# Gated scan heads: both directions as two planes of one tile per stream, queries read through a strided view

## The chip, the core and the metric

The kernel runs on one core of one Trainium2 chip. The metric is the device time of one execution in microseconds (us), the median of several runs; less is better. A profile of one execution gives the span of its instructions and what every engine did in it: PE is TensorE (matrix products), PEld its loading of weights, DVE is VectorE (elementwise work on tensors), ACT is ScalarE (activation functions, also copies), POOL is GpSimd and SP is SyncE, which here only issues DMAs.

## What is computed

Two layers of a backbone work on two streams of 256 tokens with 1024 features each: the context (its constant conditioning) and the latents. A layer is half an FFN step, a mixer with four groups of heads (differential attention, latent attention, a bidirectional gated scan, grouped attention with rotary positions) and another half FFN step. The last layer needs the context only as far as the latents read it. The change touches the scan alone. With q the queries, k the keys and logf the logarithms of the gates of one direction, a head of the scan is

```
def step(S, blk):
    qb, kb, vb, gb = blk
    G = jnp.cumsum(gb, axis=2)
    rel = jnp.where(tri, G[:, :, :, None, :] - G[:, :, None, :, :], -jnp.inf)
    att = jnp.einsum("bhtsk,bhsk->bhts", qb[:, :, :, None, :] * jnp.exp(rel), kb)
    o = jnp.einsum("bhts,bhsv->bhtv", att, vb) + jnp.einsum("bhtk,bhkv->bhtv", qb * jnp.exp(G), S)
    ...
o_f, st_f = _chunk_scan(q, fw[0], v, fw[1], s_f)
o_b, st_b = _chunk_scan(flip(q), flip(bw[0]), flip(v), flip(bw[1]), s_b)
return o_f + flip(o_b), st_f, st_b
```

that is, attention in which the product of query t and key s is weighted per feature by the product of all gates between them, once forward and once backward, and the latents go on from the state that the context left. There are four such heads per layer, with 128 features for queries and keys.

## The kernel before

Activations lie with features on the 128 partitions and the 512 tokens (context first, N = 512, S = 256) along the free axis. Dense weights are split into two parts of a shorter format, so a dense product takes three matmuls.

**The scan head** (`hgrn_head`, lines 769 to 891) computes the weighted attention as plain products. For levels b = 1, 2, 4, 8, 16, 32, 64 it takes pairs of neighbouring blocks of b tokens: queries of one block meet keys of the other, and both carry the product of the gates up to their common border. KF, KB, QF and QB are the keys and queries of the forward and of the backward direction, each a tile of 128 x 512. At a level below 32, ScalarE first copies the parts of them that meet into two tiles, MQ and MK: every second run of b elements comes from the backward tile, the others from the forward tile. TensorE multiplies MK and MQ in blocks of 32 x 32 (16 matmuls in layer 0, which the profile counts as 32), VectorE merges the blocks, which multiplies half of each of the four tiles by gate products T (`tensor_mul` in place), makes the next T for each direction, and a masked copy (`copy_predicated`) takes the level's part of the products into a tile attc. At levels 32 and 64 TensorE reads KF, KB, QF and QB themselves.

```
nc.scalar.activation(v(MQ, c0)[:, :, 0], v(QB, c0)[:, :, 0], AF.Copy)
nc.scalar.activation(v(MQ, c0)[:, :, 1], v(QF, c0)[:, :, 1], AF.Copy)
nc.scalar.activation(v(MK, c0)[:, :, 0], v(KF, c0)[:, :, 0], AF.Copy)
nc.scalar.activation(v(MK, c0)[:, :, 1], v(KB, c0)[:, :, 1], AF.Copy)
...
blocks(ps, MK, MQ)
...
nc.vector.tensor_mul(v(QF, c0)[:, :, 1], v(QF, c0)[:, :, 1], tv(TF, 0, c0))
```

Each of these instructions covers 256 elements per partition in layer 0. In layer 1 the queries of the context are not needed (c0 = 256), so copies and query merges cover 128, while the key merges still cover 256.

**The gates** (`hgrn_gate`, line 752, called from `hgrn` in `dense`, line 1227) come from the dense projections: Exp, a minimum, Ln and Exp give the sigmoid, layer 1 adds an affine step, and the keys are a product; each instruction covers 512 tokens.

**Order of the work.** `mixer` (line 1026) gives the dense products of a layer and all chains of dependent steps (head groups, attention units, scan heads) to a planner, `Weave` (line 101). It adds up a rough cost of what each engine got (`Engine.price`), runs a step of a chain when its inputs should be ready by a margin, up to four chains at a time in layer 0 and three in layer 1, and otherwise a piece of dense work. A scan head gives way at each level (the `yield` statements). `copy` (line 269) puts a copy from PSUM on ScalarE or on VectorE, whichever the planner's clocks say is behind. Then each engine works through its own queue in that order. A head's scan products use a pool of two PSUM banks, its tiles a pool of 36 slots. All instructions are issued by the helper `Engine`, so the profile puts every one of them on line 88, and the program's names tell them apart: hg0~g are tiles of a scan head of layer 0 (MQ, MK, QF, QB and others), hg0~ps its products in PSUM, hg0~T its gate products, mixin0~g the gates and keys; hg1 and mixin1 are those of layer 1.

## Time and profile before

| what | value |
|---|---|
| runs | 1996.98, 1991.06 and 1992.38 us; median 1992.38 |
| span of the profiled execution | 1989.2 us (its own time is not given apart from it) |
| busy in the span | TensorE 1943.7, VectorE 1332.2, ScalarE 908.3, GpSimd 0.2 us |
| first mixer, its scan and attention part | 410 to 775 us of the span |
| FFNs between the mixers | from 775 us on; the next stage after 1148 us |
| second mixer | 1519 to 1795 us |

A span is read from first to last instruction; the time of a run also holds what lies around it. Busy time counts an engine as busy while an instruction of it executes. [...] The releaser of a wait is the event that came last by the profile.

### The profile page before, as it was taken

The page shows a single profiled execution, that of the slowest core. Times are in us where ns is not written, and L with a number is a line of the kernel's source. Part 1 is how long each engine was busy: PE and PEld are TensorE (multiplying, and loading weights), DVE is VectorE, ACT ScalarE, POOL GpSimd, SP SyncE. Part 2 cuts the span into 40 slices and gives each one's busy share as a digit, 9 for nine tenths or more (in the row PEclk, how much of TensorE's full clock was granted, in tenths as well). Part 3 has the DMA queues.
Part 4 walks back from the last instruction along what each step waited for, and adds up shares of the span by engine and source line. Part 5 has one row for each costly group of instructions (what it writes and reads, how often), then busy time and mean ns, then how long its engine had stood idle before and what let it go on. Part 6 is the DMA issues. An engine that isn't in the chain of part 4 may idle for free.

```text
span 1989.2 us, 30652 instructions
## 1 busy us (share of the span) xinstructions
PE 1943.7 (98%) x11929; PEld 1612.7 (81%) x11929; DVE 1332.2 (67%) x2706; ACT 908.3 (46%) x1826; POOL 0.2 (0%) x4
## 2 busy tenths in 40 slices
PE   6999999999999799999999999999999999899999
PEld 5888888897777578888888898888889877689999
DVE  5688678465768957875477467676656577876554
ACT  4332223355778775322223343222235577875443
POOL 0000000000000000000000000000000000000000
PEclk9999999999999999999999999999999999999999
DMA  8565556423011102654554335465543312125564
GB/s 281 173 200 179 175 172 185 124 80 119 23 62 33 45 28 80 193 162 141 159 181 147 118 107 178 150 191 156 157 121 120 109 49 70 44 85 161 167 196 123
DMA packets 87600, 260.82 MB, mean 131 GB/s; under 512 B 9248, under 2 KB 21280, under 8 KB 87456
## 3 DMA queue, kind: packets, MB, share of 16 engines
q1 hardware_dynamic: 87456, 258.88, 41.6%
q8 instruction: 93, 1.52, 0.3%
q14 instruction: 51, 0.42, 0.1%
HBM read 257.79 MB, written 1.05 MB: 130 GB/s over the span
## 4 chain that ended last, share of the span: by engine, by line
PE 92%; ACT 3%; DVE 2%; DMA 1%; issue 0%; SPq 0%; DVEq 0%; ACTq 0%
PE ffn01~pa L88 12%; PE ffn10~pa L88 12%; PE ffn00~pa L88 10%; PE mixin0~pa L88 7%; PE ffn11~pa L88 6%; PE mixin1~pa L88 5%; PE ffn00~ps L88 3%; PE ffn10~ps L88 3%; PE ffn01~ps L88 3%; PE ffn00~pb L88 3%; PE ffn10~pb L88 3%; PE ffn01~pb L88 3%; PE mixo0~pa L88 2%; PE ffn11~pb L88 2%; PE ffn11~ps L88 2%; PE hg0~ps L88 1%
## 5 line engine op out<-in xcount | busy, mean ns | idle before, releaser
L88 ACT ACTIVATE ffn10~whi<-ffn10~raw 128x1024 fp32r<-128x1024 f32 (+1 forms) x76 | 72.0, 950 | 165.6 <-PE ffn10~pa L88 46.7
L88 ACT ACTIVATE ffn01~whi<-ffn01~raw 128x1024 fp32r<-128x1024 f32 (+1 forms) x76 | 72.0, 950 | 165.4 <-PE ffn01~pa L88 50.6
L88 ACT ACTIVATE ffn00~whi<-ffn00~raw 128x1024 fp32r<-128x1024 f32 (+1 forms) x73 | 68.7, 945 | 171.2 <-DMA ffn00~raw<-win 69.9
L88 PE MATMUL ffn01~pa<-mixo0~xh,ffn01~whi 128*128 128x512 f32 (+1 forms) x384 | 142.7, 373 | 1.2 <-ACT mixo0~xh L88 1.2
L88 PE MATMUL ffn01~pa<-mixo0~xl,ffn01~whi 128*128 128x512 f32 (+1 forms) x384 | 142.8, 372 | 0.0
L88 PE MATMUL ffn10~pa<-ffn01~xh,ffn10~whi 128*128 128x512 f32 (+1 forms) x384 | 142.6, 373 | 0.0
L88 PE MATMUL ffn10~pa<-ffn01~xl,ffn10~whi 128*128 128x512 f32 (+1 forms) x384 | 142.5, 372 | 0.0
L88 PE MATMUL ffn01~pa<-mixo0~xh,ffn01~wlo 128*128 128x512 f32 (+1 forms) x384 | 142.5, 372 | 0.0
L88 PE MATMUL ffn10~pa<-ffn01~xh,ffn10~wlo 128*128 128x512 f32 (+1 forms) x384 | 142.3, 372 | 0.0
L88 DVE TENSOR_TENSOR ffn10~wlo<-ffn10~raw,ffn10~whi 128x1024 fp32r<-128x1024 f32 (+1 forms) x76 | 82.1, 1083 | 69.5 <-ACT ffn10~whi L88 69.1
L88 DVE TENSOR_TENSOR ffn01~wlo<-ffn01~raw,ffn01~whi 128x1024 fp32r<-128x1024 f32 (+1 forms) x76 | 82.1, 1083 | 64.7 <-ACT ffn01~whi L88 64.2
L88 DVE TENSOR_TENSOR ffn11~wlo<-ffn11~raw,ffn11~whi 128x1024 fp32r<-128x1024 f32 (+2 forms) x80 | 82.5, 1038 | 58.4 <-ACT ffn11~whi L88 58.4
L88 DVE TENSOR_TENSOR ffn00~wlo<-ffn00~raw,ffn00~whi 128x1024 fp32r<-128x1024 f32 (+1 forms) x73 | 78.5, 1077 | 62.4 <-ACT ffn00~whi L88 62.3
L88 PE MATMUL ffn00~pa<-init~xh,ffn00~whi 128*128 128x512 f32 x304 | 118.8, 391 | 0.0
L88 PE MATMUL ffn00~pa<-init~xh,ffn00~wlo 128*128 128x512 f32 x304 | 118.4, 389 | 0.0
L88 PE MATMUL ffn00~pa<-init~xl,ffn00~whi 128*128 128x512 f32 x304 | 118.3, 389 | 0.0
L88 DVE SCALAR_TENSOR_TENSOR ada~g<-ffn00~adaw,cs,ada~g 128x512 f32<-128x512 f32 x168 | 115.0, 749 | 0.0
L88 ACT ACTIVATE ffn11~whi<-ffn11~raw 128x1024 fp32r<-128x1024 f32 (+2 forms) x80 | 72.4, 910 | 64.1 <-issue 29.9
L88 PE MATMUL ffn11~pa<-mixo1~xh,ffn11~whi 128*128 128x256 f32 x352 | 99.2, 283 | 2.1 <-ACT mixo1~xh L88 2.1
L88 PE MATMUL ffn11~pa<-mixo1~xl,ffn11~whi 128*128 128x256 f32 x352 | 99.5, 283 | 0.0
L88 PE MATMUL ffn11~pa<-mixo1~xh,ffn11~wlo 128*128 128x256 f32 x352 | 99.3, 283 | 0.0
L88 DVE SCALAR_TENSOR_TENSOR ada~g<-ffn01~adaw,cs,ada~g 128x512 f32<-128x512 f32 x140 | 95.8, 748 | 0.8 <-DMA ffn01~adaw<-ada_w 0.8
(567 smaller groups left out, 5190.9 us busy)
## 6 DMA issues: line engine op xcount, KB each, us to landing
ffn00~adaw<-ada_w SPq DMA_DIRECT2D x48, 512.0 KB, 3.7
ffn01~raw<-win SPq DMA_DIRECT2D x44, 512.0 KB, 4.0
ffn10~raw<-win SPq DMA_DIRECT2D x44, 512.0 KB, 3.8
ffn11~raw<-win SPq DMA_DIRECT2D x44, 512.0 KB, 4.2
ffn00~raw<-win SPq DMA_DIRECT2D x41, 512.0 KB, 4.3
ffn01~adaw<-ada_w SPq DMA_DIRECT2D x40, 512.0 KB, 3.8
ffn10~adaw<-ada_w SPq DMA_DIRECT2D x40, 512.0 KB, 3.7
norm00~adaw<-ada_w SPq DMA_DIRECT2D x16, 512.0 KB, 6.1
```

The lines of the kernel that those rows point to most:

```text
L88: return f(*a, **k)
```

## The change

It keeps gates, keys and queries of a head in tiles of two planes, one per direction, and one such tile per stream of 256 tokens: FF (gates), KK (keys) and QQ (queries; here the backward direction is the first plane). A view `skew(t, b)` takes every second run of b elements from the second plane and the others from the first, so what MQ and MK held is now one view of QQ or KK. The queries are read by TensorE through that view and are not copied any more. The keys are still copied, one copy per stream that is needed: two of 256 elements in layer 0 and one of 256 in layer 1. The merges, too, go through the view: one for the keys and one for the queries of each stream, 256 elements each. Both directions' T are one tile and one product. The gates' last step, the keys, the sum of the keys k0 and the first query products are made per stream, in halves. `view`, a new helper, builds an access pattern by hand. Comments and docstrings are removed; this is left out here.

```diff
+    def view(self, t, off, *dims):
+        return bass.AP(t.tensor, t.offset + off, [t.ap[0], *dims])
...
-        nc.scalar.activation(f, f, AF.Exp, scale=-1.0)
+        for o, cc in outs or [(f, slice(None))]:
+            nc.scalar.activation(o, f[:, cc], AF.Exp, scale=-1.0)
...
         if l:
-            nc.vector.scalar_tensor_tensor(k, k, a, f, ALU.mult, ALU.mult)
-            nc.scalar.activation(f, f, AF.Identity, bias=b, scale=a)
+            self.sigmoid(e, f, ps)
+            for s, cc in enumerate(streams):
+                nc.vector.scalar_tensor_tensor(KK[s][:, d], e[:, cc], a, f[:, cc], ALU.mult, ALU.mult)
+                nc.scalar.activation(FF[s][:, d], f[:, cc], AF.Identity, bias=b, scale=a)
         else:
-            nc.vector.tensor_mul(k, k, f)
+            self.sigmoid(e, f, ps, [(FF[s][:, d], cc) for s, cc in enumerate(streams)])
+            for s, cc in enumerate(streams):
+                nc.vector.tensor_mul(KK[s][:, d], e[:, cc], FF[s][:, d])
...
+        QQ = {s: self.g([P, 2, S]) for s in streams}
+        for s in streams:
+            cc = slice(s * S, (s + 1) * S)
+            nc.vector.tensor_add(k0[:, cc], KK[s][:, 0], KK[s][:, 1])
+            for i in range(2):
+                nc.vector.tensor_mul(QQ[s][:, i], q[:, cc], FF[s][:, 1 - i])
+        def skew(t, b, off=0, n=S):
+            return self.view(t, off, [2 * b, n // (2 * b)], [S + b, 2], [1, b])
...
             if b < 32:
-                MQ, MK = self.g([P, N]), self.g([P, N])
-                nc.scalar.activation(v(MQ, c0)[:, :, 0], v(QB, c0)[:, :, 0], AF.Copy)
-                nc.scalar.activation(v(MQ, c0)[:, :, 1], v(QF, c0)[:, :, 1], AF.Copy)
-                nc.scalar.activation(v(MK, c0)[:, :, 0], v(KF, c0)[:, :, 0], AF.Copy)
-                nc.scalar.activation(v(MK, c0)[:, :, 1], v(KB, c0)[:, :, 1], AF.Copy)
+                MK = self.g([P, N])
+                for s in streams:
+                    x = MK[:, s * S:(s + 1) * S].rearrange("p (n two b) -> p n two b", two=2, b=b)
+                    nc.scalar.activation(x, skew(KK[s], b), AF.Copy)
...
-                blocks(ps, MK, MQ)
+                blocks(ps, whole(MK), lambda t, j: skew(QQ[t // 2], b, t % 2 * P + j, 32))
...
-            nc.vector.tensor_mul(v(KF)[:, :, 0], v(KF)[:, :, 0], tv(TF, 1))
-            nc.vector.tensor_mul(v(KB)[:, :, 1], v(KB)[:, :, 1], tv(TB, 0))
-            nc.vector.tensor_mul(v(QF, c0)[:, :, 1], v(QF, c0)[:, :, 1], tv(TF, 0, c0))
-            nc.vector.tensor_mul(v(QB, c0)[:, :, 0], v(QB, c0)[:, :, 0], tv(TB, 1, c0))
+            for s in (0, 1):
+                src, o1, pl = (FF[s], 0, S) if b == 1 else (T, s * nb // 2, nb)
+                dims = [2, S // (2 * b)], [0, b]
+                x = skew(KK[s], b)
+                nc.vector.tensor_mul(x, x, self.view(src, o1 + 1, dims[0], [pl - 1, 2], dims[1]))
+                if s in streams:
+                    x = skew(QQ[s], b)
+                    nc.vector.tensor_mul(x, x, self.view(src, o1 + 1 + pl, dims[0], [-pl - 1, 2], dims[1]))
```

By the order of both kernels TensorE has 10632 instructions in each, VectorE 2708 before and 2665 now, and ScalarE 1710 before and 1621 now. SyncE and GpSimd issue the same. ScalarE's queue, at a level of 16 of the last scan head of layer 0 (hg0~g_6880 and 6881 are MQ and MK before, hg0~g_6796 is MK now; g_6416, 6415 are query tiles, mixin0~g key tiles), before:

```order
L88 ACTIVATE hg0~g_6847<-hg0~ps_6848 128x512
L88 ACTIVATE hg0~g_6880<-hg0~g_6416 128x16x16
L88 ACTIVATE hg0~g_6880<-hg0~g_6415 128x16x16
L88 ACTIVATE hg0~g_6881<-mixin0~g_6244 128x16x16
L88 ACTIVATE hg0~g_6881<-mixin0~g_6251 128x16x16
L88 ACTIVATE gqa0~g_6887<-mixin0~pa_6737 128x384
```

and now:

```order
L88 ACTIVATE hg0~g_6737<-hg0~ps_6738 128x512
L88 ACTIVATE ffn10~s_13030<-ffn10~s_13030 128x2
L88 ACTIVATE mixin0~g_5737<-hg0~pb_6760 64x512
L88 ACTIVATE hg0~g_6796<-mixin0~g_5747 128x256
L88 ACTIVATE hg0~g_6796<-mixin0~g_5748 128x256
L88 ACTIVATE y1~g_6799<-da0~g_5901 128x512
```

Four copies of 16 runs of 16 elements have become two of 256 elements, and those for the queries are gone.

VectorE's queue around the merges of that level, before (g_6416 and 6415 are the two query tiles, mixin0~g the two key tiles, hg0~T the gate products; a row's last part names the counter that it waits for):

```order
L88 TENSOR_TENSOR hg0~g_6416<-hg0~g_6416,hg0~T_6877 128x16x16 [waits Activation_49]
L88 TENSOR_TENSOR hg0~g_6415<-hg0~g_6415,hg0~T_6875 128x16x16 [waits Activation_49]
L88 TENSOR_TENSOR mixin0~g_6244<-mixin0~g_6244,hg0~T_6875 128x16x16 [waits Activation_49]
L88 TENSOR_TENSOR mixin0~g_6251<-mixin0~g_6251,hg0~T_6877 128x16x16 [waits Activation_49]
L88 TENSOR_REDUCE gqa0~s_6890<-gqa0~g_6887 128x6 [waits Activation_49]
L88 TENSOR_TENSOR t1mrope_13079<-sm_13065,cst 128x64
L88 SCALAR_TENSOR_TENSOR t2mrope_13080<-sm_13065,cst 128x2x16
L88 TENSOR_TENSOR t2mrope_13080<-sm_13065,cst 128x2x16
L88 TENSOR_TENSOR ffn10~s_13095<-sm_13065 128x32 x2
L88 COPY_PREDICATED hg0~attc_6512<-msk,hg0~ps_6920 128x128 [waits DVE_49,PE_49]
```

and now (mixin0~g_5747 and 5748 are the keys of the context and of the latents, hg0~g_6361 and 6362 their queries; the rows begin with the merges of the level of 8):

```order
L88 TENSOR_TENSOR mixin0~g_5747<-mixin0~g_5747,hg0~T_6731 128x16x2x8 [waits Activation_49]
L88 TENSOR_TENSOR hg0~g_6361<-hg0~g_6361,hg0~T_6731 128x16x2x8 [waits PE_49]
L88 TENSOR_TENSOR mixin0~g_5748<-mixin0~g_5748,hg0~T_6731 128x16x2x8 [waits Activation_49]
L88 TENSOR_TENSOR hg0~g_6362<-hg0~g_6362,hg0~T_6731 128x16x2x8 [waits PE_49]
L88 COPY_PREDICATED hg0~attc_6436<-msk,hg0~ps_6772 128x128
L88 TENSOR_TENSOR ffn10~s_13027<-sm_12997 128x32
L88 TENSOR_REDUCE ffn10~s_13030<-ffn10~s_13027 128x2 [waits DVE_49]
L88 TENSOR_TENSOR nlam_13033<-ffn10~s_13030 128x1 [waits Activation_49]
L88 TENSOR_SCALAR nlam_13033<-nlam_13033 128x1 [waits DVE_49]
L88 TENSOR_TENSOR mixin0~g_5747<-mixin0~g_5747,hg0~T_6793 128x8x2x16 [waits Activation_49]
L88 TENSOR_TENSOR mixin0~g_5748<-mixin0~g_5748,hg0~T_6793 128x8x2x16 [waits Activation_49]
L88 TENSOR_TENSOR hg0~g_6361<-hg0~g_6361,hg0~T_6793 128x8x2x16 [waits PE_49]
```

The query merges waited for ScalarE's copies and now wait for TensorE (PE). At the level of 8 the key merge of the second stream stands behind the query merge of the first; at 16 both key merges come first. The masked copy now comes behind the merges of its level and, in the row shown, has no wait of its own.

## Rows read from the trace of the kernel before

**Rows 1.** The page of the profile: span, and busy time of TensorE.
```profile
span 1989.2 us, 30652 instructions
...
PE 1943.7 (98%) x11929; PEld 1612.7 (81%) x11929; DVE 1332.2 (67%) x2706; ACT 908.3 (46%) x1826; POOL 0.2 (0%) x4
```

**Rows 2.** Windows: length, busy PE, PEld, DVE, ACT, POOL (count), PEclk, DMA, GB/s.
```profile
410.00:775.00 365.00, 352.15 (x2834) 276.08 (x2834) 259.79 (x719) 257.35 (x656) 0.00 (x0) 0.99 0.19 59
775.00:1148.00 373.00, 372.63 (x1788) 308.85 (x1789) 244.52 (x396) 118.26 (x170) 0.00 (x0) 1.00 0.48 150
1519.00:1795.00 276.00, 263.47 (x1968) 210.90 (x1968) 200.32 (x554) 200.87 (x520) 0.00 (x0) 0.99 0.24 77
```

**Rows 3.** What TensorE waited for, 410 to 775 us: total, times, longest.
```profile
PE gqa0~pb L88 <- DVE gqa0~g L88: 3.8, 1, 3.8
PE hg0~ps L88 <- ACT hg0~g L88: 3.0, 1, 3.0
```

**Rows 4.** Busy time in the four stretches where TensorE idles.
```profile
640.00:694.00 54.00, 43.28 (x517) 30.82 (x515) 48.63 (x152) 44.13 (x117) 0.00 (x0) 0.94 0.14 42
1696.00:1714.00 18.00, 14.74 (x147) 10.64 (x147) 15.08 (x51) 14.62 (x42) 0.00 (x0) 0.91 0.01 5
1726.00:1738.00 12.00, 7.20 (x71) 4.61 (x70) 10.06 (x38) 9.81 (x33) 0.00 (x0) 0.96 0.43 130
1750.00:1768.00 18.00, 16.23 (x152) 11.35 (x151) 13.03 (x39) 15.99 (x40) 0.00 (x0) 1.00 0.03 4
```

**Rows 5.** The same, where the granted clock (PEclk) falls.
```profile
676.00:682.00 6.00, 3.46 (x40) 2.47 (x41) 4.99 (x18) 3.85 (x11) 0.00 (x0) 0.74 0.24 81
688.00:694.00 6.00, 5.09 (x48) 4.12 (x49) 6.00 (x25) 5.47 (x13) 0.00 (x0) 0.72 0.19 74
1702.00:1714.00 12.00, 9.64 (x99) 6.62 (x100) 9.63 (x33) 10.50 (x31) 0.00 (x0) 0.86 0.00 1
1732.00:1744.00 12.00, 9.59 (x80) 7.54 (x81) 9.30 (x31) 7.14 (x26) 0.00 (x0) 0.86 0.15 46
```

**Rows 6.** Groups, ScalarE's scan copies: count, busy us, mean ns, idle before, releaser.
```profile
L88 ACT ACTIVATE hg0~g<-hg0~g 128x256 f32<-128x256 f32 x40 | 15.0, 423 | 1.8 <-DVE hg0~g L88 1.8
...
L88 ACT ACTIVATE hg1~g<-hg1~g 128x128 f32<-128x128 f32 x40 | 10.6, 311 | 3.3 <-DVE hg1~g L88 3.2
```

**Rows 7.** Groups, ScalarE: an Exp of 512 and of 256 elements, second mixer.
```profile
L88 ACT ACTIVATE mixin1~g<-mixin1~g 128x512 f32<-128x512 f32 x8 | 5.0, 621 | 0.0
...
L88 ACT ACTIVATE mixin1~g<-mixin1~g 128x256 f32<-128x256 f32 x6 | 2.4, 407 | 0.0
```

**Rows 8.** Groups, VectorE: merges and masked copies, both mixers.
```profile
L88 DVE TENSOR_TENSOR mixin0~g<-mixin0~g,hg0~T 128x256 f32<-128x256 f32 x48 | 18.7, 421 | 3.4 <-PE hg0~ps L88 3.3
...
L88 DVE COPY_PREDICATED hg0~attc<-msk,hg0~ps 128x128 f32<-128x128 uint8 x20 | 6.0, 301 | 1.5 <-PE hg0~ps L88 1.4
...
L88 DVE TENSOR_TENSOR mixin1~g<-mixin1~g,hg1~T 128x256 f32<-128x256 f32 x48 | 19.0, 420 | 2.9 <-PE hg1~ps L88 2.7
L88 DVE TENSOR_TENSOR hg1~g<-hg1~g,hg1~T 128x128 f32<-128x128 f32 x48 | 12.3, 286 | 1.8 <-ACT hg1~g L88 1.8
...
L88 DVE COPY_PREDICATED hg1~attc<-msk,hg1~ps 128x64 f32<-128x64 uint8 x20 | 4.6, 228 | 5.9 <-PE hg1~ps L88 5.8
```

**Rows 9.** Groups, scan copies in 640 to 694 and 1696 to 1714 us.
```profile
L88 ACT ACTIVATE hg0~g<-mixin0~g 128x256 f32<-128x256 f32 x18 | 6.6, 422 | 0.0
L88 ACT ACTIVATE hg0~g<-hg0~g 128x256 f32<-128x256 f32 x17 | 6.5, 420 | 0.7 <-DVE hg0~g L88 0.7
...
L88 ACT ACTIVATE hg1~g<-mixin1~g 128x128 f32<-128x128 f32 x8 | 2.0, 307 | 0.0
```

**Rows 10.** Instructions in order of time: the products of one level.
```profile
669.61 0.46 PE L88 MATMUL hg0~ps<-hg0~g,hg0~g 128*32 128x32 f32 x32
```

**Rows 11.** One tile's instructions, 410 to 775 us: ns min/median/max.
```profile
L88 DVE TENSOR_TENSOR hg0~g<-hg0~g,hg0~T x48: 416/420/437, 504.8 to 704.6; 128x256 f32<-128x256 f32 x48
...
L88 DVE TENSOR_TENSOR hg0~g<-hg0~g,mixin0~g x8: 419/421/421, 503.5 to 671.2; 128x256 f32<-128x256 f32 x8
```

More of the change, by code (lines that the diff above doesn't have):

```diff
@@ L737, in tokmajor, with sigmoid @@
             then(tt, ps)
[L739 removed]
+    def sigmoid(self, e, f, x, outs=None):
         nc = self.nc
@@ L750, in silu, with hgrn_q, hgrn_gate, hgrn_head @@
         self.nc.vector.tensor_mul(out, out, ps)
-    def hgrn_gate(self, l, h, i, ps, c0):
-        nc = self.nc
-        f = self.g([P, N])
-        if i == 0:
-            self.silu(f[:, c0:], ps[:, c0:])
-            return f
-        k = self.g([P, N])
-        self.sigmoid(k, f, ps)
-        if l:
-            a, b = self.oml[:, i - 1, h:h + 1], self.lb[:, i - 1, h:h + 1]
-            nc.vector.scalar_tensor_tensor(k, k, a, f, ALU.mult, ALU.mult)
-            nc.scalar.activation(f, f, AF.Identity, bias=b, scale=a)
-        else:
-            nc.vector.tensor_mul(k, k, f)
-        return f, k
-    def hgrn_head(self, l, h, q, F, K, o, last):
+    def hgrn_q(self, ps, c0):
+        q = self.g([P, N])
+        self.silu(q[:, c0:], ps[:, c0:])
+        return q
+    def hgrn_gate(self, l, h, d, ps, FF, KK):
+        nc = self.nc
+        e, f = self.g([P, N]), self.g([P, N])
+        streams = [slice(s * S, (s + 1) * S) for s in range(2)]
+        if l:
+            self.sigmoid(e, f, ps)
+            a, b = self.oml[:, d, h:h + 1], self.lb[:, d, h:h + 1]
+            for s, cc in enumerate(streams):
+                nc.vector.scalar_tensor_tensor(KK[s][:, d], e[:, cc], a, f[:, cc], ALU.mult, ALU.mult)
+                nc.scalar.activation(FF[s][:, d], f[:, cc], AF.Identity, bias=b, scale=a)
+        else:
+            self.sigmoid(e, f, ps, [(FF[s][:, d], cc) for s, cc in enumerate(streams)])
+            for s, cc in enumerate(streams):
+                nc.vector.tensor_mul(KK[s][:, d], e[:, cc], FF[s][:, d])
+    def hgrn_head(self, l, h, q, FF, KK, o, last):
         nc = self.nc
@@ L834, in hgrn_head @@
-            nT = []
-            for T in (TF, TB):
-                T2 = self.sp.tile([P, nb // 2], F32, tag=f"T{b}", name=self.nm("T"), bufs=3 if b < 4 else 4)
-                tt_ = T[:, :nb].rearrange("p (n two) -> p n two", two=2)
-                nc.vector.tensor_mul(T2, tt_[:, :, 0], tt_[:, :, 1])
-                nT.append(T2)
-            TF, TB = nT
+            for s in (0, 1):
[6 more added lines that the diff above has]
+                    nc.vector.tensor_mul(x, x, self.view(src, o1 + 1 + pl, dims[0], [-pl - 1, 2], dims[1]))
@@ L841, in hgrn_head @@
+            if b == 1:
+                T2 = self.g([P, 2, nb // 2])
+            else:
+                T2 = self.sp.tile([P, 2, nb // 2], F32, tag=f"T{b}", name=self.nm("T"), bufs=2)
+            for s in (0, 1) if b == 1 else (None,):
+                x = (T if s is None else FF[s]).rearrange("p d (n two) -> p d n two", two=2)
+                nc.vector.tensor_mul(T2 if s is None else T2[:, :, s * P:s * P + P], x[:, :, :, 0], x[:, :, :, 1])
+            T = T2
             if b < 32:
@@ L852, in hgrn_head @@
         ps = self.pss([P, 4, P])
[L853 removed]
         for a in range(t0, 4, 2):
[L855 to L856 removed]
+            mm(ps[:, a], K(0, a), Q(0, a + 1), start=True, stop=True)
+            mm(ps[:, a + 1], K(1, a + 1), Q(1, a), start=True, stop=True)
         self.copy(cross[:, t0:], ps[:, t0:])
[L859 to L862 removed]
+        for x, d, t in ((Q(0, 3), 0, 2), (Q(1, 2), 1, 3), (K(0, 0), 0, 1), (K(1, 1), 1, 0)):
+            nc.vector.tensor_scalar_mul(x, x, T[:, d, t:t + 1])
         yield
@@ L867, in hgrn_head @@
         for s in range(2):
-            mm(ps[:, s], KF[:, sl(s)], QF[:, S:], start=True, stop=False)
-            mm(ps[:, s], KB[:, sl(s)], QB[:, S:], start=False, stop=True)
+            for d in range(2):
+                mm(ps[:, s], K(d, s), QQ[1][:, 1 - d], start=d == 0, stop=d == 1)
         self.copy(cl, ps)
@@ L878, in hgrn_head @@
         po = self.psb()[r]
+        c0 = t0 * P
+        sl = lambda t: slice(t * P, (t + 1) * P)
         v = lambda t: self.vi[:, t, S + 64 * h:S + 64 * h + 64]
@@ L1235, in hgrn @@
                     self.hg_tiles += 1
-                    tiles.append(self.hgrn_gate(l, h, i, ps, c0))
+                    if i == 0:
+                        tiles[:] = [self.hgrn_q(ps, c0)] + [[self.g([P, 2, S]) for _ in range(2)] for _ in range(2)]
+                    else:
+                        self.hgrn_gate(l, h, i - 1, ps, *tiles[1:])
                     if i == 2:
@@ L1241, in hgrn @@
                                 self.headnorm(f"y{4 + n}", o, self.hgn, c0, gates, n)))
-                        q, (ff, fk), (bf, bk) = tiles
-                        del tiles[:]
                         self.hg_open += 1
-                        W.spawn(self.hgrn_head(l, h, q, [ff, bf], [fk, bk], Y[4 + h // 2], last))
+                        W.spawn(self.hgrn_head(l, h, *tiles, Y[4 + h // 2], last))
                         self.ph = ph
```

48 lines of the change are left out of this document (16 added, 32 removed).

## The prediction

> **What bounds the kernel now.** I read the span and the engines' shares first: TensorE is busy 1943.7 us of a span of 1989.2 us [rows 1]. The profiled execution's own time is not given apart from its span; the median of the three timed runs, 1992.38 us, lies 3.2 us above it, so I work out a change of the span and add 3.2 us. Next the stretches by stage [rows 2]: in an FFN between the mixers (775 to 1148 us) TensorE is busy 372.63 of 373 us, and nothing that ScalarE or VectorE gain there can shorten it. In the mixers (410 to 775 and 1519 to 1795 us) it idles 365 - 352.15 = 12.9 us and 276 - 263.47 = 12.5 us. These 25.4 us are what the change can win, with what the clock loses beside them. The waits of TensorE in the mixers [rows 3] end on VectorE and on ScalarE alike; the second longest of the first mixer (3.0 us) is for a scan copy of ScalarE. Nearly all of the idle time lies in four stretches [rows 4]: 54 - 43.28 = 10.7 us in the first mixer, and 3.3, 4.8 and 1.8 us, together 9.8 us, in the second. There both other engines are near full: in the first VectorE has 48.63 of 54 us and ScalarE 44.13; in the last ScalarE has 15.99 of 18. [...]
>
> **What the change removes and adds.** TensorE's instructions are the same in number and size (the order of both kernels has 10632), so no matmul work goes.
>
> ScalarE, copies. A level below 32 had four copies of 256 elements in layer 0 (two for the queries, two for the keys) and four of 128 in layer 1. Over five levels and four heads that is 80 of 0.42 us and 80 of 0.31 us [rows 6] (each row stands for two groups of 40). They become 40 and 20 of 256 elements: 80 x 0.42 - 40 x 0.42 = 16.8 us less in layer 0, 80 x 0.31 - 20 x 0.42 = 16.4 us less in layer 1 (busy times of single ones; they overlap by a sixth in a row, so some 12 us of engine time each).
>
> ScalarE, gates. The last Exp of layer 0 and the affine step of layer 1 come in halves: two of 256 for one of 512, 2 x 0.407 - 0.621 = 0.19 us more [rows 7], 16 times, 3 us. What hides them is TensorE's dense work: outside of the four stretches it idles only 25.4 - 20.5 = 4.9 us in both mixers. I count them at nothing, and at +3.0 us if that cover is gone.
>
> VectorE. Layer 0 has as many merges of 256 elements as before; a level's two products of T become one (some ten small ones fewer per head in both layers, a few us in all), and k0, the query products and the keys are made in halves, which gives about as much back. By the order VectorE also takes over some ten copies from PSUM in layer 0. So layer 0 is about even. In layer 1 two query merges of 128 become one of 256: 2 x 0.286 - 0.421 = 0.15 us less per level [rows 8], 24 times, 3.6 us, and with T about 6 us of 200.
>
> The new wait. The merged queries are no longer a copy: TensorE reads them in place, so the merge that overwrites them has to wait until this level's products are done. Before, only the masked copy into attc waited for them, and the merge could run ahead. Behind the waiting merge in VectorE's queue stand the other stream's key merge (and with it ScalarE's next copy), the masked copy, and whatever chain comes next; whoever needs those waits too. The nearest rows are the merges at 32 and 64, which read in place already [rows 8]: VectorE idled 3.3 us for the products ahead of them in layer 0 and 2.7 us in layer 1, over 8 levels each, 0.38 us per level. Against that stands what the masked copies waited, 1.4 and 5.8 us over 20 levels each, 0.18 us, which falls away since they now come behind the merges. Net 0.2 us per level.
>
> How many levels count: 35 copies lie in the first stretch [rows 9], about 9 levels; with the same density the other 48 us hold 8. Outside of the 17 the wait costs nothing, as TensorE is full there.
>
> **The sum.** (a) First mixer, 640 to 694 us: 35 copies of 13.1 us are halved, 6.6 us of ScalarE. VectorE's load stays, so at most its idle 54 - 48.63 = 5.4 us can go; I take half, -2.7. (b) Second mixer: in 1696 to 1714 us 16 copies of 4.0 us (two groups of 8 [rows 9]) become four of 0.42, -2.3 or so; the other two stretches lose what the whole mixer loses, 16.4 of 200.87 us or 8%, of their 9.81 + 15.99 = 25.8 us of ScalarE, -2.1, and VectorE loses 6 of 200.32 us, 3%, of its 38.2 us in the three, -1.2. The sum is 5.6 us, of 9.8 us that could go; the engines' parts overlap, so -5.0. (c) One of the four falls of the clock does not come: -1.7 (0 to -6.6). (d) The new wait, 17 x 0.2: +3.3, with ends of 0 and of 18.7: a product group takes 0.46 us [rows 10], and with three dense matmuls of 373/1788 = 0.21 us queued ahead of it a level would wait 1.1 us. (e) The strided reads of TensorE, VectorE and ScalarE: taken at 0, as VectorE's merges of level 1, of every second element, cost 419 to 421 ns, and those of all longer runs 416 to 437 [rows 11]; the other end stands under the rivals. Together -6.1 us: a span of 1983.1 us, a time of **1986.3 us**. The ends of the terms give -5.4 - 9.8 - 6.6 = -21.8 (1970.6 us) and, with no gain, +18.7; neither is likely whole.
>
> **Rivals.** *Nothing that counts.* VectorE is 90% busy in the long stretch [rows 4] and its load there does not fall; then (a) is nothing, (b) is halved and eaten by (d), and the time is 1992 us. For it speaks that the longest wait, 3.8 us, is on VectorE; against it, that ScalarE has the last stretch nearly full.
>
> *Slower: the merge behind the products.* Mechanism and place: VectorE's queue at levels 1 to 16 in the four stretches, price as in (d). The gains (a) to (c) are 9.4 us, so it decides from 9.4/17 = 0.55 us per level on. With one product group and three dense matmuls, 1.1 us, it is 18.7 - 9.4 = +9.3: 2001.7 us. For it: one in-order queue serves up to four chains, and at one level in the second excerpt of the order the key merge of stream 1 stands behind the query merge of stream 0. Against it: elsewhere both key merges are put ahead, and the rows that wait already paid 0.38 us.
>
> *Each element from another plane.* At level 1 the new view takes one element from one plane and the next from the other. The closest reads of before are of every second element, and cost what long runs cost [rows 11]; none jumps at each element. If each element then took two accesses, a merge of 256 would cost 256 x (0.421 - 0.286)/128 = 0.27 us more: 28 merges at level 1 give 7.6 us, 12 copies by 256 x (0.42 - 0.31)/128 = 0.22 us 2.6 us, of which 17 of 40 levels, 4.3 us, are in the four stretches; 8 product groups of 0.46 us doubled are 3.7 us, and TensorE is always on the path. With the forecast's gain that is 1986.3 + 8.0 = 1994.3 us. [...]
>
> *That the change does not do what it says* I rule out: the order has 40 and 20 copies where there were 80 and 80.
>
> **How the numbers follow.** About 0.3%, 6 us, is what a measurement here can tell from no change. Chances: forecast 0.56, nothing 0.19, slower by the merge 0.19, planes 0.06. The forecast's own range is 1976 to 1991 us, as every term is a half of something; the order of all chains moves too, which can shift a wait by a few us either way. The forecast lies at the edge of 0.3% (1986.4), and its upper end is nearer to it than its lower: two thirds of it, 0.38, and a little of the others are faster: 0.41. Within 0.3%: a third of the forecast, 0.17, most of nothing, 0.13, and most of the planes and the milder end of the slower case, 0.06: 0.36. Slower: 0.23. The range over all cases, 1975 to 2001 us, leaves out the best tenth and the worst tenth.
>
> **What would show it.** Right: 60 ScalarE copies in place of 160 at 0.42 us; PE idle in the two mixers down from 25.4 to about 19 us, with the fall in the second mixer larger; at least one fall of the clock gone; VectorE's idle ahead of the scan's query merges some 0.4 us per level, and almost none ahead of the masked copies. Wrong: waits on PE's scan products in front of VectorE of 0.6 us or more per level (the slower rival); merges or copies of level 1 over 0.6 us, or groups of 32 matmuls well above 0.46 us (planes); VectorE over 90% in the tail with PE idle as before (nothing). It is also wrong if dense stretches change, which no term here moves.

## The result, and the profile after

The changed kernel takes 2015.1 us (median; 2014.27 to 2018.35) against 1992.51 us for the kernel before in the same comparison: a ratio of 1.0112, interval 1.0097 to 1.0126, so 22.6 us slower. The forecast was 1986.3 us and the range ended at 2001 us. The page of the changed kernel, span and busy times:

```profile
span 2013.3 us, 30575 instructions
...
PE 1961.3 (97%) x11929; PEld 1623.9 (81%) x11929; DVE 1334.9 (66%) x2663; ACT 891.2 (44%) x1737; POOL 0.2 (0%) x4
```

TensorE has as many matmuls as in [rows 1], but is busy 17.6 us longer; ScalarE has 89 instructions and 17.1 us less, VectorE 43 instructions less and about the same time. To see where the span grew I cut each mixer into three stretches: from the first to the last dense input product (mixin), from there to the first output product (mixo), and the output products. Two views of windows, length, busy time of PE, PEld, DVE, ACT and POOL with the number of records, granted clock (PEclk, the share of its full speed that TensorE was given), DMA share and GB/s; before first, then after; three lines per mixer:

```profile
409.20:670.30 261.10, 257.98 (x2065) 204.26 (x2066) 186.82 (x503) 189.70 (x492) 0.00 (x0) 1.00 0.18 58
670.30:691.30 21.00, 12.89 (x224) 9.49 (x222) 19.34 (x68) 15.57 (x42) 0.00 (x0) 0.87 0.30 94
691.30:767.80 76.50, 76.20 (x509) 57.48 (x509) 47.60 (x136) 48.22 (x116) 0.00 (x0) 0.99 0.17 56
1518.10:1726.60 208.50, 204.45 (x1460) 163.61 (x1460) 151.06 (x418) 150.46 (x389) 0.00 (x0) 0.99 0.23 73
1726.60:1741.30 14.70, 9.90 (x98) 6.63 (x96) 11.22 (x42) 11.68 (x40) 0.00 (x0) 0.88 0.31 93
1741.30:1790.40 49.10, 47.31 (x409) 39.44 (x407) 35.02 (x92) 36.47 (x88) 0.00 (x0) 1.00 0.27 87
```

```profile
408.80:664.90 256.10, 254.06 (x1955) 200.84 (x1954) 178.16 (x468) 171.92 (x436) 0.00 (x0) 0.99 0.19 60
664.90:705.10 40.20, 31.83 (x423) 22.20 (x421) 35.62 (x122) 25.06 (x67) 0.00 (x0) 0.70 0.14 45
705.10:780.00 74.90, 72.12 (x423) 54.01 (x422) 44.82 (x116) 46.81 (x110) 0.00 (x0) 1.00 0.17 57
1530.20:1740.20 210.00, 205.53 (x1433) 164.96 (x1432) 146.22 (x371) 143.80 (x346) 0.00 (x0) 0.97 0.23 72
1740.20:1756.60 16.40, 9.21 (x119) 6.75 (x118) 14.64 (x46) 9.70 (x30) 0.00 (x0) 0.70 0.28 81
1756.60:1814.40 57.80, 53.54 (x414) 43.24 (x413) 34.69 (x90) 38.22 (x88) 0.00 (x0) 0.97 0.22 74
```

The first mixer grew from 358.6 to 371.2 us, and more than all of it is in the middle stretch, 40.2 us where there were 21.0; the other two are shorter. The second grew from 272.3 to 284.2 us, mostly in its output products, 57.8 us for 49.1. The FFNs did not change: from the end of the first mixer to the start of the second it is 750.2 us, before 750.3. The records tell what happened: in the middle stretch of the first mixer TensorE has 423 instead of 224, and the stretch ahead of it has 110 fewer and the one behind it 86 fewer. Work of the chains that had lain between dense products came to stand where there are no dense products left.

It costs in two ways. Over the three stretches of the first mixer TensorE is busy 358.01 us for 347.07 with the same number of records (2801 and 2798): 10.9 us more, and 1.7 us more idle time. In the second it is 268.28 for 261.66 us: 6.6 us more, and 5.3 us more idle time. Together that is 17.5 + 7.0 = 24.5 us, where the two profiled spans differ by 24.1 and the medians by 22.6. I put the longer busy time down to the clock, and the granted clocks leave room for that. In the changed kernel dense input products of 128 x 512 start every 0.43 us where the clock is 0.50 (five between 1723.8 and 1725.6 us) and every 0.23 us where it is 1.00 (17 between 1727.1 and 1730.9 us). By that a stretch loses, as an estimate, at most its length times what is missing from a clock of 1: in the first mixer 0.01 x 256.1 + 0.30 x 40.2 = 14.6 us, before 0.13 x 21.0 + 0.01 x 76.5 = 3.5; in the second 0.03 x 210.0 + 0.30 x 16.4 + 0.03 x 57.8 = 13.0 us, before 0.01 x 208.5 + 0.12 x 14.7 = 3.8. The view of windows in the changed kernel's first mixer shows the clock falling:

```profile
656.00:662.00 6.00, 6.00 (x63) 4.09 (x61) 5.60 (x18) 5.13 (x13) 0.00 (x0) 1.00 0.03 6
662.00:668.00 6.00, 4.47 (x50) 3.06 (x48) 5.57 (x14) 5.43 (x15) 0.00 (x0) 1.00 0.40 129
668.00:674.00 6.00, 3.95 (x44) 2.33 (x44) 5.63 (x16) 3.36 (x10) 0.00 (x0) 0.50 0.37 102
674.00:680.00 6.00, 5.53 (x87) 4.38 (x87) 5.78 (x15) 3.21 (x9) 0.00 (x0) 0.50 0.14 53
680.00:686.00 6.00, 4.56 (x26) 2.52 (x24) 5.55 (x20) 3.58 (x11) 0.00 (x0) 0.57 0.19 76
686.00:692.00 6.00, 4.44 (x80) 3.68 (x81) 5.96 (x28) 4.67 (x12) 0.00 (x0) 0.71 0.01 3
692.00:698.00 6.00, 5.84 (x67) 4.42 (x65) 4.72 (x26) 3.02 (x9) 0.00 (x0) 0.72 0.00 0
```

TensorE was busy 4.47 of 6 us in 662 to 668 us, and then stood at a granted clock of 0.50 for 12 us and for parts of the 18 us behind them. In the kernel before, the falls of [rows 5] were shorter: windows of 1 us show two or three in a row at 0.50 (679 to 682, 690 to 692, 1707 to 1709 and 1737 to 1740 us) and partial ones beside them, 3.4 us at 0.50 in each fall. In the second mixer the longest fall comes before the dense input products run out (at 1740.2 us), so there it is not only the tail that starves TensorE:

```profile
1711.00:1717.00 6.00, 3.50 (x23) 1.73 (x23) 5.78 (x18) 4.27 (x13) 0.00 (x0) 0.63 0.01 3
1717.00:1723.00 6.00, 4.88 (x54) 3.60 (x54) 5.95 (x20) 4.86 (x13) 0.00 (x0) 0.50 0.00 1
```

The groups that answer to [rows 6, 8], in the first mixer (to 790 us) and then in the second (to 1830 us):

```profile
L88 ACT ACTIVATE hg0~g<-mixin0~g 128x256 f32<-128x256 f32 x40 | 15.8, 440 | 2.5 <-DVE mixin0~g L88 2.5
...
L88 DVE TENSOR_TENSOR hg0~g<-hg0~g,hg0~T 128x256 f32<-128x256 f32 x40 | 16.1, 418 | 2.7 <-PE hg0~ps L88 2.6
...
L88 DVE COPY_PREDICATED hg0~attc<-msk,hg0~ps 128x128 f32<-128x128 uint8 x20 | 5.8, 292 | 0.0
...
L88 DVE TENSOR_TENSOR hg0~g<-hg0~g,mixin0~g 128x256 f32<-128x256 f32 x8 | 4.9, 637 | 0.6 <-PE hg0~ps L88 0.6
```

```profile
L88 ACT ACTIVATE hg1~g<-mixin1~g 128x256 f32<-128x256 f32 x20 | 8.8, 442 | 2.4 <-DVE mixin1~g L88 2.4
...
L88 DVE TENSOR_TENSOR hg1~g<-hg1~g,hg1~T 128x256 f32<-128x256 f32 x20 | 8.4, 420 | 6.7 <-PE hg1~ps L88 6.6
...
L88 DVE COPY_PREDICATED hg1~attc<-msk,hg1~ps 128x64 f32<-128x64 uint8 x20 | 4.5, 223 | 0.0
```

Sixty copies are left, at 0.44 us. The query merges idle 2.6 and 6.6 us for TensorE's products (hg~ps), and the masked copies, which idled 1.4 and 5.8 us, idle no more. At level 1 a merge now takes 0.637 us, where T is still the tile of the gates.

### The profile page after: what moved, and what is told of

It is laid out like the page before. It is cut to its first block, busy times and chain, and to the rows that moved or that the text cites. A ratio compares the mean times of both kernels' runs of the same rounds, so it can differ in the third digit from the quotient of the medians.

```text
span 2013.3 us, 30575 instructions
## 1 busy us (share of the span) xinstructions
PE 1961.3 (97%) x11929; PEld 1623.9 (81%) x11929; DVE 1334.9 (66%) x2663; ACT 891.2 (44%) x1737; POOL 0.2 (0%) x4
## 4 chain that ended last, share of the span: by engine, by line
PE 92%; DVE 3%; ACT 3%; DMA 1%; issue 1%; SPq 0%; DVEq 0%
PE ffn01~pa L88 12%; PE ffn10~pa L88 12%; PE ffn00~pa L88 10%; PE mixin0~pa L88 7%; PE ffn11~pa L88 6%; PE mixin1~pa L88 5%; PE ffn00~ps L88 3%; PE ffn10~ps L88 3%; PE ffn01~ps L88 3%; PE ffn00~pb L88 3%; PE ffn10~pb L88 3%; PE ffn01~pb L88 3%; PE mixo0~pa L88 2%; PE ffn11~pb L88 2%; PE ffn11~ps L88 2%; PE hg0~ps L88 1%
```

## Experiments

Three theories were set against each other: A, the query merge that waits for the products; B, the order: a planner that is told of a cheaper scan mixes chains and dense work in another way (with the order goes, through `copy`, the engine of some copies from PSUM; both together are the plan here); C, the alternating planes of level 1. The lengths of the mixers from first input to last output product stand beside each time (before: 358.6 and 272.3 us; changed: 371.2 and 284.2 us), and what the order has left after the last dense input product: scan products (ps), products of differential attention (da), and, for the second mixer, the output products behind the last output of a scan head (out). Before, it is 144 ps, 8 da in the first and 70 ps, 12 da, 85 out in the second; in the change 176, 44 and 84, 12, 131. Ratios are against the kernel before.

### The plan of before, the plan of after

In both kernels the planner can be told other costs than those of the instructions that it issues. The first run issues the instructions of the change at the prices of before, the second those of before at the prices of the change:

```diff
+    def planned(self, real, *ops):
+        cost = self.nc.cost
+        saved = dict(cost)
+        r = real()
+        cost.update(saved)
+        for kind, n in ops:
+            cost[kind] += 0.06 + n / 960.0 if kind == "dve" else 0.07 + n / 1200.0
+            if cost["last"] != kind:
+                cost["last"] = kind
+                cost["hops"] += 1
+        return r
...
+                self.planned(merged, *[("act", W // 2)] * 4)
...
+            T = self.planned(merges, ("dve", S), ("dve", S), ("dve", W // 2), ("dve", W // 2), ("dve", nb // 2), ("dve", nb // 2))
```

> The changed kernel, but the planner is told the costs that the scan had before (engine, elements and number of instructions), so that it makes the choices of the kernel before; the instructions are those of the change. Theory A (the query merges wait for TensorE's products, and what stands behind them is late): the wait is in every level still, so the time stays near the 2015 us of the change, 2008 to 2020. Theory B (the order: with a cheaper scan the planner mixes dense products and chains in another way, and TensorE starves in the tails): back to the 1992.5 us of before, 1986 to 1999, with no stretch of half clock longer than 7 us. Theory C (merges, copies and reads of level 1, whose neighbours lie in different planes, 0.637 us against 0.420 us per merge): stays, 2008 to 2020.

Measured: 1998.97 us, ratio 1.0027 (1.0016 to 1.0038); mixers 361.4 and 274.3 us. By the order 160 ps and 12 da are left in the first tail, and 70, 12 and 85 in the second, as before. Of 22.6 us 6 are left, and the time lies just inside what B gave. In the mixers the falls of the clock, of which B allowed none over 7 us, are as it said too: the longest of the first mixer was 2 x (0.23 + 0.50 + 0.41) x 3 = 6.8 us, if the clock was either 0.50 or 1.00 all along, by the three rows below (length first, granted clock third from the end).

```profile
679.00:682.00 3.00, 1.31 (x35) 0.87 (x22) 3.00 (x10) 0.85 (x4) 0.00 (x0) 0.77 0.03 5
682.00:685.00 3.00, 1.57 (x36) 1.45 (x37) 3.00 (x10) 2.89 (x8) 0.00 (x0) 0.50 0.52 153
685.00:688.00 3.00, 3.00 (x10) 1.73 (x9) 1.82 (x7) 0.86 (x2) 0.00 (x0) 0.59 0.00 0
```

> The kernel before, but the planner is told the costs that the scan has after the change; the instructions are those of before. Theory A (wait of the query merges) and theory C (level 1 across planes): 1988 to 1998 us, as neither the wait nor the planes are there. Theory B (the order): near the change, 2008 to 2020 us, with the granted clock of a mixer's tail at 0.5 for 10 us or more in a row.

Measured: 2015.45 us, ratio 1.0109 (1.0089 to 1.0129); mixers 365.3 and 285.6 us. The kernel before is as slow as the changed one once it is planned at the new prices, with its instructions as they were but for five copies from PSUM, which the plan moved from ScalarE (1821 instructions for 1826) to VectorE (2711 for 2706). Its middle stretches, and below them a fall of the clock in its second mixer:

```profile
660.30:699.80 39.50, 27.99 (x415) 20.44 (x413) 32.97 (x111) 27.90 (x78) 0.00 (x0) 0.83 0.16 51
...
1735.00:1752.60 17.60, 9.11 (x135) 6.79 (x134) 16.44 (x58) 11.94 (x42) 0.00 (x0) 0.76 0.23 76
...
1710.00:1720.00 10.00, 7.38 (x58) 4.49 (x57) 8.64 (x29) 8.62 (x21) 0.00 (x0) 0.50 0.00 0
```

The tail is 39.5 us long with 415 records, as in the change. In this tail the clock falls less than I had expected (two falls of 6.8 us each, worked out in the same way from windows of 3 us in 666 to 687 us), and more of the loss is idle time, 39.50 - 27.99 = 11.5 us; the 10 us in a row at 0.5 that B gave are there in the second mixer, but ahead of its last dense input product. The two runs settle between B and the rest: the plan alone makes all of the difference in the medians (22.4 of 22.6 us; in the profiled executions the two mixers together grow by 20.0 of 24.5 us), and under the plan of before A and C can hold no more than what was left in the first run, 6 us. What they hold under the new plan the next runs ask.

### The queries copied again

```diff
+                MQ = self.g([P, N])
+                for s in streams:
+                    x = MQ[:, s * S:(s + 1) * S].rearrange("p (n two b) -> p n two b", two=2, b=b)
+                    self.planned(lambda: nc.scalar.activation(x, skew(QQ[s], b), AF.Copy))
...
-                blocks(ps, whole(MK), lambda t, j: skew(QQ[t // 2], b, t % 2 * P + j, 32))
+                blocks(ps, whole(MK), whole(MQ))
```

> The changed kernel with one thing put back: ScalarE copies the queries of a level below 32 through the view, one copy per stream, and TensorE reads the copy, so that the query merge need not wait for the products. The planner is not told of these 60 copies. Theory A (the wait): the 2.6 + 6.6 us that VectorE idles ahead of those merges go, and with them the starving of the tails: 2004 us or less. Theory B (the order): 2010 to 2020 us, as the plan is that of the change. Theory C: 2010 to 2020 us, 12 more copies of level 1 included.

Measured: 2018.46 us, ratio 1.0129 (1.0111 to 1.0147); mixers 368.5 and 284.2 us. The same edit on the run with the plan of before:

> The changed kernel with the planner told the costs of before (that run took 1999.0 us, 6 us above the kernel before), and the queries copied by ScalarE again, so that the query merges need not wait for the products. Theory A (what is left, 6 us, is the wait of the merges): 1994 us or less. Rival D (it is the order that is left, 160 scan products in the first tail against 144, and the level-1 planes): 1997 to 2001 us.

Measured: 2001.03 us, ratio 1.0033 (1.0021 to 1.0045); mixers 366.7 and 275.2 us. With either plan nothing comes back (the first mixer of the second run is even 5.3 us longer than without the copies), so theory A falls as the cause of the 22 us. What the wait costs by itself the runs do not tell, as ScalarE has 60 copies more in them. Where the wait went can be read in VectorE's waits in the second mixer (engine, tile and its releaser: us in total, times, longest), first with the plan of before and the queries read in place, then copied:

```profile
DVE hg1~g L88 <- PE hg1~ps L88: 4.4, 13, 0.8
DVE mixin1~g L88 <- PE hg1~ps L88: 3.8, 7, 0.9
```

```profile
DVE hg1~attc L88 <- PE hg1~ps L88: 3.6, 10, 1.0
DVE mixin1~g L88 <- PE hg1~ps L88: 3.0, 5, 1.0
```

4.4 us ahead of the query merges become 3.6 us ahead of the masked copies. The masked copy of a level needs the same products; the change only moved the point at which VectorE stops for them by a few instructions.

### Level 1 in one plane

```diff
-            return self.view(t, off, [2 * b, n // (2 * b)], [S + b, 2], [1, b])
+            return self.view(t, off, [2 * b, n // (2 * b)], [1 if b == 1 else S + b, 2], [1, b])
```

(and the same for the views of the gates).

> The changed kernel, but at level 1 the views of keys, queries and gates are a run of 256 neighbouring elements of one plane in place of every second element from each plane; number and size of the instructions stay, and what level 1 computes is not the reference's. Merges of level 1 should take 0.42 us in place of 0.637 us. Theory C (level 1 across planes): 28 merges times 0.21 us are 6 us of VectorE, and the time falls by 6 us or more, to 2009 us or less. Theories A and B: within 4 us of 2015 us.

Measured: 2015.77 us, ratio 1.0114 (1.0098 to 1.0129); mixers 369.6 and 283.1 us. Again the same edit with the plan of before:

> The changed kernel with the planner told the costs of before (1999.0 us), and the views of level 1 as a run of neighbouring elements of one plane; what level 1 computes is not the reference's. Theory C (what is left, 6 us, are the reads and writes across planes at level 1): 1995 us or less. Rivals A and D: 1997 to 2001 us.

Measured: 1995.57 us, ratio 1.0014 (1.0005 to 1.0023); mixers 359.2 and 273.7 us, 2.2 and 0.6 us shorter than in the run without the edit. The merges of level 1 (the rows x8 that read mixin0~g) did what was said; the view of a tile, ns min/median/max, of the changed kernel, with the key copies of all levels and, in the last row, the query merges of level 2, and then of the first of the two runs:

```profile
L88 ACT ACTIVATE hg0~g<-mixin0~g x40: 397/418/530, 502.5 to 700.8; 128x256 f32<-128x256 f32 x40
...
L88 DVE TENSOR_TENSOR hg0~g<-hg0~g,mixin0~g x8: 610/638/664, 504.8 to 679.2; 128x256 f32<-128x256 f32 x8
...
L88 DVE TENSOR_TENSOR hg0~g<-hg0~g,hg0~g x8: 417/418/427, 515.7 to 686.9; 128x256 f32<-128x256 f32 x8
```

```profile
L88 DVE TENSOR_TENSOR hg0~g<-hg0~g,mixin0~g x8: 413/420/426, 505.6 to 679.1; 128x256 f32<-128x256 f32 x8
```

Theory C has its mechanism and its price, 28 x 0.22 = 6 us of VectorE, but with the plan of the change the time does not move. With the plan of before it comes to 3.4 us at the median, between what C and what its rivals gave; the two intervals overlap (1.0016 to 1.0038, 1.0005 to 1.0023), and of the 4.7 us between the two profiled spans 2.0 lie ahead of the first mixer (it starts at 411.7 and at 409.7 us), where the edit does nothing.

### Which prices, and other plans

If the order decides, part of the prices should bring part of the time back. In the next run only the copies are priced as before; in the two behind it, those of both layers, with the other prices of before in layer 1 as well, and then without the copies in layer 1.

```diff
+                self.planned(merged, *[("act", nt * P // 2)] * 4)
```

> The changed kernel, but the planner is told the four copies per level of before in place of the two or one that are issued; all other costs are those of the change. By the order this puts the first mixer's tail back (after the last dense input product 144 scan products and 8 of differential attention are left, as in before; the change leaves 176 and 44), and not the second's (92 scan products left, 70 in before; 131 output products behind the last scan's output, 85 in before). Theory B1 (the price of the copies moves the order, and the work left over when the dense products run out sets the tail): the first mixer ends 5 to 8 us earlier against its start than in the changed kernel, the second as late as there: 2002 to 2010 us. Rival B2 (only the whole set of prices matters, the count of left products tells nothing): both mixers as in the change, 2012 to 2019 us.

Measured: 2002.23 us, ratio 1.0045 (1.0029 to 1.0061); mixers 358.6 and 283.3 us. The first mixer is as long as before, to a tenth of a microsecond (B1 had said 5 to 8 us shorter, it is 12.6), and the second still as in the change, as B1 had it. Its first middle stretch:

```profile
672.00:689.50 17.50, 12.50 (x224) 9.01 (x223) 17.12 (x53) 12.68 (x34) 0.00 (x0) 0.90 0.15 50
```

> The changed kernel; the planner is told the price of the copies of before in both layers, and in layer 1 that of the gates, first products and merges of before as well. By the order both tails hold what they hold in the kernel before (144 scan products and 8 of differential attention in the first, 70 and 12 in the second). If the order is the cause, and each mixer keeps its own: the first mixer as in the run with the copies priced alone (1 us over before), the second as in the run with all prices of before (2 us over): 1994 to 1999 us. If the order is not the cause: 2005 us or more.

Measured: 1995.5 us, ratio 1.0007 (0.9998 to 1.0016); mixers 358.8 and 273.7 us. With the tails filled as before, the changed kernel is as fast as the kernel before, within what can be told apart, and no faster. Its first middle stretch:

```profile
675.00:691.80 16.80, 12.44 (x223) 9.12 (x222) 16.80 (x53) 12.57 (x34) 0.00 (x0) 0.90 0.17 52
```

> As the run before it, but in layer 1 the planner is not told the price of the copies. By the order the second tail holds 84 scan products and 26 of differential attention, and 67 output products stand behind the last scan output (85 in before, 131 in the change). If the output products that are left behind the last scan output tell the end of the second mixer: 1990 to 1998 us. If a plan other than the tuned one costs whatever those counts are: 2000 us or more.

Measured: 2006.58 us, ratio 1.0065 (1.0046 to 1.0084); mixers 358.4 and 284.0 us. Fewer output products behind the last scan output did not help; my count was no measure of the second mixer's end. Two runs change a number of the planner and nothing else, on the changed kernel:

```diff
-WEAVE = ((4, 2.0, 2.0, 0.1), (3, 2.0, 8.5, 0.15))
+WEAVE = ((4, 1.0, 2.0, 0.1), (3, 2.0, 8.5, 0.05))
```

> The changed kernel with two numbers of the planner changed: margin 1.0 in place of 2.0 in layer 0, price of a hop 0.05 in place of 0.15 in layer 1. By the order the first tail has 96 scan products and none of differential attention left (176 and 44 in the change, 144 and 8 before), the second 84 and 85 output products behind the last scan output (84 and 131 in the change). If the work left in the tails sets the time: 1985 to 2000 us. If a smaller margin brings waits into the dense part, or the count of products left tells nothing: 2005 us or more.

Measured: 2021.05 us, ratio 1.0137 (1.012 to 1.0154); mixers 380.7 and 283.5 us. The slowest of all, with the emptiest first tail. The windows show why:

```profile
409.50:691.70 282.20, 273.57 (x2181) 210.80 (x2180) 193.18 (x510) 187.17 (x475) 0.00 (x0) 0.98 0.17 53
691.70:712.70 21.00, 14.04 (x202) 10.78 (x201) 19.80 (x64) 11.83 (x32) 0.00 (x0) 0.80 0.21 62
```

The middle stretch is back at 21.0 us, but the dense part before it takes 282.2 us for 256.1. It holds 226 records more, and TensorE idles 282.20 - 273.57 = 8.6 us in it, for 2.0 in the change, as it would if chain steps were issued before their inputs are there; that this is the reason is not shown.

> The changed kernel with the planner's margin at 2.5 in place of 2.0 in both layers, no other number changed. By the order 128 scan products and none of differential attention are left in the first tail, 100 and 30 in the second, 86 output products behind the last scan output. If the tail alone decides: 1990 to 2002 us; if the numbers of the planner fit one set of costs only: 2005 to 2025 us.

Measured: 2005.97 us, ratio 1.0059 (1.0045 to 1.0073); mixers 363.0 and 279.7 us: 9 us faster than the changed kernel at a margin of 2.0, though no faster than the kernel before. And the same margin on the kernel before:

```diff
-WEAVE = ((4, 2.0, 2.0, 0.1), (3, 2.0, 8.5, 0.15))
+WEAVE = ((4, 2.5, 2.0, 0.1), (3, 2.5, 8.5, 0.15))
```

> The kernel before with the planner's margin at 2.5 in place of 2.0 in both layers; its instructions are the same in number and size. If the planner's numbers sit at a point that was found for just these costs, any step away costs as much as the change did: 2000 to 2025 us. If the order matters only through the change's own instructions: within 6 us of 1993 us.

Measured: 2011.99 us, ratio 1.0089 (1.0075 to 1.0103); mixers 371.0 and 276.9 us. Half a microsecond more margin costs the unchanged kernel 18.6 us, most of what the change cost.

```profile
409.30:678.00 268.70, 261.26 (x1987) 206.51 (x1986) 186.44 (x491) 188.03 (x485) 0.00 (x0) 0.99 0.18 56
678.00:694.90 16.90, 6.23 (x202) 3.87 (x201) 16.90 (x58) 13.62 (x39) 0.00 (x0) 0.72 0.39 120
694.90:780.30 85.40, 84.19 (x610) 63.12 (x610) 53.38 (x159) 52.36 (x126) 0.00 (x0) 0.98 0.15 50
```

The dense part, 268.7 us for 261.1, and the output products, 85.4 for 76.5, are longer here, and the middle stretch is shorter (16.9): the same work lies in other places again.

### Level 1 through one plane after the other

```diff
-            return self.view(t, off, [2 * b, n // (2 * b)], [S + b, 2], [1, b])
+            d = [2 * b, n // (2 * b)], [S + b, 2]
+            return self.view(t, off, *(d[::-1] if b == 1 and n == S else d), [1, b])
...
-                nc.vector.tensor_mul(x, x, self.view(src, o1 + 1, dims[0], [pl - 1, 2], dims[1]))
+                    turn = lambda *d: (*(d[::-1] if b == 1 else d), dims[1])
+                    nc.vector.tensor_mul(x, x, self.view(src, o1 + 1, *turn(dims[0], [pl - 1, 2])))
```

> The changed kernel with the mixed prices (that run took 1995.5 us), and at level 1 the merges and key copies walk through one plane first (every second element of it) and then through the other; the same elements, in another sequence, TensorE's reads as they were. Merges of level 1 should take 0.42 us in place of 0.63 us, as every second element of one tile did before. If the alternation of planes at each element is what is left of the cost (3 us between the run of 1999.0 us and that of 1995.6 us with one plane): 1991 to 1994 us, as the kernel before or just under it. If that was the order again: 1995 to 1998 us.

Measured: 1994.77 us, ratio 1.0002 (0.9993 to 1.0011); mixers 358.1 and 274.7 us. The merges fell as expected:

```profile
L88 DVE TENSOR_TENSOR hg0~g<-hg0~g,mixin0~g x8: 420/426/429, 508.1 to 675.4; 128x256 f32<-128x256 f32 x8
```

Against the run with the mixed prices (1.0007) the gain can't be told from nothing. Whether the last 2 us of that run were the planes, the order or neither stays open; they are below what the measurement resolves. No version that was run is faster than the kernel before.

## Why the prediction was wrong

**The step that failed** is a half sentence under how the numbers follow: that the order of all chains moves too, "which can shift a wait by a few us either way". I read the order for what the change does to single levels, and held the plan around them to be the same. But the instructions' prices are the planner's input. Told of cheaper scan steps it made an order that runs out of dense products with 176 scan products and 44 of differential attention to go instead of 144 and 8. That was worth 22 us (2015.45 us with the instructions of before), against "a few". Why a cheaper step leaves more work for the tail, and not less, no run shows; the price of the copies alone puts the first mixer's tail back, and the second's needs the other prices as well. The two orders could have been counted as wholes, and rows of single levels could not show this.

**What bounds the kernel**: right as far as it went. With the plan of before, the change's instructions left TensorE's dense stretches as they were (261.6 us for 261.1, and 208.2 for 208.5), and the 25.4 us of idle time in the mixers were the place to look. But I took that idle time as what the change could win, and not as what it could grow: the tails are as long as the plan makes them.

**(a), (b) ScalarE's copies**: the count was right, 60 for 160, at 0.44 for 0.42 us. The gain was not there. With the tails filled as before (mixed prices) the first mixer takes 358.8 us for 358.6 and the second 273.7 for 272.3, where I had -2.7 and -5.0 us. What the rival "nothing that counts" said, VectorE full in the tail, fits in the first mixer: in its middle stretch VectorE is busy 19.34 of 21.0 us before, and in the run with the mixed prices all of 16.80 us. In the second mixer's (11.22 of 14.7 us before) it is not full, and why nothing was gained there stays open.

**(c) The clock**: I had one fall less, 1.7 us. No run shows this term, nor the 6.6 us of its far end; in its place the runs show longer falls (0.50 from 668 to 685 us in the first mixer of the changed kernel, where those of before have 3.4 us each), and dense products that start every 0.43 us in such a fall and every 0.23 us outside of it. In the profiled executions TensorE was busy 17.5 us longer, the largest part of the loss, and the granted clocks leave room for all of it. In both kernels the falls lie in and behind stretches in which TensorE idles (it was busy 4.47 of 6 us ahead of the longest), and the sign followed those stretches.

**(d) The new wait**: 3.3 us in the forecast, with an end at 18.7. VectorE's wait for the products is there (2.6 and 6.6 us ahead of the query merges), and what the masked copies no longer wait stands against it, as I said. (They stood behind the merges before, too; what is new is that a merge ahead of them waits.) Taken together, VectorE's waits for the scan products in the two mixers were 15.1 us before and 16.3 in the run with the change's instructions and the plan of before: 1.2 us more over 40 levels, 0.03 us per level where I had 0.2. In the changed kernel, with its own plan, they were 21.0. Copying the queries again brought nothing back under either plan. So the rival on the slow side had the right sign and the wrong cause: its wait is not what made the kernel slower.

**(e) The planes**: taken at 0; a merge of level 1 took 0.637 us for 0.420, 0.22 us more, where the rival had 0.27. A copy of level 1 took up to 0.530 us against a median of 0.418, half of the rival's 0.22. TensorE's products did not double, but they do pay. The view of the tile hides it:

```profile
L88 PE MATMUL hg0~ps<-hg0~g,hg0~g x640: 192/196/263, 504.4 to 701.4; 128*32 128x32 f32 x160
```

Only a fifth of these records read level 1 through the view, so the median is that of the other levels. In order of time, the products of levels 1 and 2 of one head (two records for each product), first in the run with the plan of before and then in the same with level 1 in one plane:

```profile
540.09 0.54 PE L88 MATMUL hg0~ps<-hg0~g,hg0~g 128*32 128x32 f32 x32
547.56 0.46 PE L88 MATMUL hg0~ps<-hg0~g,hg0~g 128*32 128x32 f32 x32
```

```profile
537.90 0.46 PE L88 MATMUL hg0~ps<-hg0~g,hg0~g 128*32 128x32 f32 x32
544.99 0.46 PE L88 MATMUL hg0~ps<-hg0~g,hg0~g 128*32 128x32 f32 x32
```

The price is 0.08 us for a group of 32 at level 1, where the rival had 0.46. For VectorE the runs show 0.421 us for every second element of one plane [rows 11], 0.638 us where each element comes from the other plane, 0.418 us at level 2, where two neighbours come from each plane, and 0.426 us for the elements of level 1 walked one plane after the other. So its price goes with the sequence and not with the elements. That an element then takes two accesses was the rival's assumption, and no run shows it; TensorE pays in the same place, at a far smaller price.

## What to carry to other kernels

Where a planner or scheduler sets the order from costs, an edit that makes an instruction cheaper is also an edit of the order. Compare the two orders as wholes first (what stands behind the last piece of cover work), and test the plan apart from the instructions, by telling each kernel's planner the other's costs: two runs settled here what no row of the trace could. A planner's numbers go with one set of costs: half a microsecond more margin took 9 us off the changed kernel and put 18.6 on the kernel before. After a change they are to be searched again, and by running, since neither count that I tried foretold the time once a plan was other than that of before. And a median over a mixed group says nothing of a fifth of it; ask for the instructions themselves.

## What the runs showed of the hardware

In the two mixers TensorE was busy 17.5 us longer with as many matmuls, with a granted clock of 0.70 in place of 0.87 in the middle stretch of the first (40.2 us in place of 21.0) and of 0.70 in place of 0.88 in that of the second. A stretch short of dense work was paid twice here, as idle time (7.0 us more in the two mixers) and as a granted clock of 0.50 in it (668 to 685 us in the first mixer); at that clock the dense products of the second mixer started every 0.43 us, at 1.00 every 0.23.

At 256 elements VectorE took 0.64 us when neighbours came alternately from two places 257 elements (1028 bytes) apart, and 0.42 us for the same elements in another sequence. ScalarE's copies took up to 0.53 us in place of 0.42 when they read that way, and TensorE's 16 products of a level 0.54 us in place of 0.46.
